# One encoder layer on one core: the first norm by wide VectorE operations, the first modulation rows behind the eighth state-space pair, and the up pass's input factors two attention blocks sooner

## The chip, the cores and the metric

The kernel runs on one core of a Trainium2 chip. A core has five engines with an instruction queue each: TensorE (PE: matmuls, with PEld for its weight loads), VectorE (DVE), ScalarE (ACT), GpSimd (POOL) and SyncE (SP), which here only issues DMAs. Every engine works through its own queue in order, and an instruction whose operand is not ready holds back all that is queued behind it. The metric is device time in microseconds (us); less is better.

## The reference, cut to what matters

One layer (depth 1), 2048 positions, 1024 channels, one sequence:

```
mod = c @ w_ada + b_ada                       # six rows of 1024: shift, scale, gate, twice
h = rms_norm(x, g_pre_mix) * (1 + sc_m) + sh_m
u, f, q, k, v = split(h @ w_in)
y = concat(s5_mixer(u), fourier_mixer(f), window_attention(q, k, v)) @ w_out
x = x + gt_m * rms_norm(y, g_post_mix)
h = rms_norm(x, g_pre_ffn) * (1 + sc_f) + sh_f
gate, val = split(dwconv3(h @ w_up))
x = x + gt_f * rms_norm((gelu(gate) * val) @ w_down, g_post_ffn)
```

The s5 mixer is a diagonal complex state-space scan over 24 channel groups in two directions with a gated output. The attention sees 128 positions to either side, with 6 query heads on 2 key heads.

## The kernel before, in words

**Layout and precision.** Channels lie on the 128 partitions, in 8 chunks of 128; positions are the free axis, mostly in four chunks c of 512. Large products run in split fp16: a value is written as HI + LO, and a product takes three matmuls (HI*HI, LO*HI, HI*LO). So what feeds TensorE is made twice, as a HI by ScalarE and as a LO (the value less its HI) by VectorE.

**Order of the work.** Nothing is ordered by hand. Each step is a Python generator (a process) that asks for an engine with an assumed cost and a ready time; `Sched` (line 121) is a greedy planner: of all processes that could go it takes the one that can start earliest on the planned clocks, ties going to the smaller priority number, and lets it emit its instruction. Each engine's queue gets its order from those planned times. `("w", future)` makes a process wait in the plan until another has set the future; `("acq", sem, n)` takes places of a limited resource, a PSUM bank for example. Such a gate is no instruction: it only decides how early in the queues the steps behind it stand. The planner books a VectorE tensor_tensor at 0.07 + 0.00105 us per element of a partition and a GpSimd one at 0.07 + 0.0022 us. It knows nothing of engines that slow each other down.

**Buffers.** All working tiles (`u`, 4 KB for each partition) come out of one pool of 50. PSUM has three groups of banks: z (3), s (4), m (1).

**Stages.**
1. Modulation: `mod_scale` (line 359) makes the first scale by matmuls, `mod_shift` (line 394) makes the first shift by eight wide multiply-and-sum rows on VectorE. When both are there for channel chunk k, the future `f_as[k]` is set.
2. First norm, `norm_x(c)` (line 479), for c = 0 to 3: four loads of x, squares on ScalarE, sums, a matmul by ones and an inverse root (`rnorm`, line 344). Then for each k the value x * r * a1 + s1 is made and split into HI and LO. For an even k this is `affine_split` (line 464): two VectorE scalar_tensor_tensor and one ScalarE activation of 512 each. For an odd k it is `affine_split2` (line 471): a GpSimd tensor_tensor by r, two ScalarE activations and a VectorE subtraction. `f_h[k][c]` is set when both halves lie there. Chunks 1 to 3 wait for `f_as[7]`.
3. The input projection (`ustream`, `zstream`) reads these halves; the constants of the s5 mixer (`s5_consts`, line 728) are made on VectorE, GpSimd and ScalarE next to it.
4. Twelve s5 pairs, prepared by `s5_prep` and run by two `s5_chain` processes (line 954). Pair b sets `f_yd[b]`.
5. The other 32 modulation rows, `mod_rest` (line 430). Each is one 512 KB load by SyncE (line 265) and one VectorE multiply-and-sum of 1024 (line 444), at the lowest priority. Rows 0 to 7 give `gm` (used by `proj`), 8 to 15 `s2`, 16 to 23 `a2` (used by `post`, which waits for `f_modr`), 24 to 31 `gf` (used at the end). Rows 8 to 23 wait for `f_yd[7]`, rows 24 to 31 for the first output projection tile; with `G_M1 = 0` rows 0 to 7 wait for nothing but `f_as[7]`.
6. Fourier mixer, gate of the s5 output, and attention in 16 blocks by two workers (`att`, line 1275; block n sets `f_ya[n]`), all of attention's matmuls in s banks. Output projection `proj` (line 1412) for c = 0 to 3, each needing four attention blocks, and `post` (line 1474), the second norm, which sets `f_hp[c]`.
7. The up pass (`ffn`, line 1652) in two halves p of the positions. The convolution is folded into a fast product scheme with seven products for each weight; `hcomb(p)` (line 1562) makes the seven input factors H of half p: per half 8 wide VectorE sums or differences and 14 HI and LO splits of 2 x 512. For p = 0 it waits for `f_hp[0]` and `f_hp[1]`, and, as `H_GATE = 1`, for `f_ya[15]`, the last attention block. `ffn` then walks over 22 weight tiles; for each it takes a place, two `u` tiles (line 1678) and an s bank, and only then waits for its H factor. The first weights are prepared after `f_pc[0]`, the end of the first output projection chunk's matmuls.
8. The down pass, of the same product scheme, and the last norm.

Lines 270, 275, 282, 284, 289, 305 and 316 are the helpers that emit ScalarE activations, tensor_tensor, tensor_scalar (282 and 284), scalar_tensor_tensor, memset and matmuls. All steps share them, so the profile is read by time and shape more than by line.

Of the kernel before, what the change touches and what calls it, by code (L numbers as in the profile page):

```python
# [12 lines left out]
AF = mybir.ActivationFunctionType  # L13
ALU = mybir.AluOpType
X = mybir.AxisListType.X

P = 128
# [20 lines left out]
HI, LO = 0, 1  # L38
# [4 lines left out]
PK = 100  # L43
S5_MUL = "V"
S5_ADD = "V"
G_M1 = 0
POST_B = 0.0
S5_B = 0.0
ATT_B = 0.0
# [20 lines left out]
N_SL = 3  # L70
W_ADD, H_ADD, G_ADD, SSQ = "VVVV", "V", "VVVV", "V"
W_LEAD, W_RAW, U_PAIRS, D_LEAD, TAIL = 3, 1, 4, 6, 2
F_GATE, H_GATE, D_FROM = 0, 1, (1, 0, 2)
N_CH = 2
N_PE = (1,)
G_M2 = 8
# [126 lines left out]
class Builder:  # L203
# [257 lines left out]
                self.f_gf.set(t)  # L461


    def affine_split(self, t, x, r, a, b, hi, lo):

        t = yield from self.stt(t, x, x, a, r, ALU.mult, ALU.mult)
        t = yield from self.act(t, hi, x, AF.Identity, bias=b)
        t = yield from self.stt(t, lo, x, b, hi, ALU.add, ALU.subtract)
        return t

    def affine_split2(self, t, x, r, a, b, hi, lo):

        t = yield from self.tt(t, x, x, r, ALU.mult, eng="G")
        t = yield from self.act(t, hi, x, AF.Identity, scale=a, bias=b)
        t = yield from self.act(t, x, x, AF.Identity, scale=a, bias=b)
        t = yield from self.tt(t, lo, x, hi, ALU.subtract)
        return t

    def norm_x(self, c, slots):
        t0 = yield ("acq", slots, 1)  # L480
        if c:
# [1 line left out]
        xs, tx = [], []  # L483
        for q in range(4):
            x = self.u([2, 512])
# [3 lines left out]
        for q in range(4):  # L489
            sq.append(self.u([2, 512]))  # L490
            if (c, q) in SQ_G:
                t = yield from self.tt(tx[q], sq[q], xs[q], xs[q], ALU.mult, eng="G")
            else:
                t = yield from self.act(tx[q], sq[q], xs[q], AF.Square)
# [6 lines left out]
        if c not in N_PE:  # L501
            acc = sq[0]
            t = yield from self.tt(max(ts_), acc, acc, sq[2], ALU.add)
            t = yield from self.stt(t, acc[:, 0], acc[:, 0], DELTA, acc[:, 1], ALU.add, ALU.add)
            parts = [(t, acc[:, 0])]
        rt = self.u([2, 512])
        tr = yield from self.rnorm(parts, 512, rt[:, 0], rt[:, 1])
        h = self.h[c] = [[self.u([4, 512], F16) for _ in range(2)] for _ in range(2)]
        for q in range(4):
            for k in (2 * q, 2 * q + 1):  # L510
                ta = yield ("w", self.f_as[k])
                ta = yield from (self.affine_split2 if k % 2 else self.affine_split)(
                    max(tr, ta), xs[q][:, k % 2], rt[:, 0], self.a1[:, k:k + 1], self.s1[:, k:k + 1],
                    h[HI][k // 4][:, k % 4], h[LO][k // 4][:, k % 4])
                self.f_h[k][c].set(ta)
        slots.give(ta)
        if c:
# [1044 lines left out]
    def hcomb(self, p):  # L1562
# [1 line left out]
        for i in range(2):  # L1564
            yield ("w", self.f_hp[2 * p + i])
        (ya, ta), (yb, tb) = self.f_hp[2 * p].val, self.f_hp[2 * p + 1].val
        if p == 0 and H_GATE:
            yield ("w", self.f_ya[15])
        H = self.H[p] = {}
        if p:  # L1570
            self.f_ht = {r: [Fut(), Fut()] for r in (1, 5, 6, 2, 7, 3, 4)}
# [80 lines left out]
    def ffn(self):  # L1652
# [10 lines left out]
        self.f_wd = [Fut() for _ in range(11)]  # L1663
        self.sc.spawn(self.down_weights(), 4)
        pairs = Sem(U_PAIRS)
        for p in range(2):
            fH = self.f_H[2 * p]
            gos = {}
# [4 lines left out]
            for i in range(NFF):  # L1673
# [22 lines left out]
                t = yield ("acq", self.bank["s"], 1)  # L1696
                b1 = self.ps("s")
                t = yield from prod(1, b1, max(t, tp), True)
                self.sc.spawn(self.up_copy(t, b1, U[0][:, n0], f[1]))
                t = yield ("acq", self.bank["s"], 1)  # L1700
                b2 = self.ps("s")
                t = yield from prod(5, b2, t, True)
                self.sc.spawn(self.up_copy(t, b2, U[1][:, n1], f[5]))
                t = yield ("w", f[1])
                t = yield from prod(6, b1, t, False)
                self.sc.spawn(self.up_copy(t, b1, U[0][:, n1], f[6]))
                t = yield ("acq", self.bank["z"], 1)
                b3 = self.ps("z")
                t = yield from prod(2, b3, t, True)
                self.sc.spawn(self.up_add(t, b3, U[0][:, n0], f[1], f[2], True))  # L1710
                t = yield ("w", f[6])
                t = yield from prod(7, b1, t, False)
                self.sc.spawn(self.up_add(t, b1, U[1][:, n1], f[5], f[7], False))
                t = yield ("w", f[5])
                t = yield from prod(3, b2, t, False)
                self.sc.spawn(self.up_add(t, b2, U[0][:, n1], f[6], f[3], True))
                t = yield ("w", f[7])
# [392 lines left out]
```

## Time and profile before

| what | us |
| --- | --- |
| median of 3 runs | 2134.07 (2133.83 to 2138.75) |
| the profiled execution | 2141.4 |
| its span, first to last instruction | 2139.6 |
| TensorE busy in the span | 1963.9 (92%) |
| VectorE busy | 1559.8 (73%) |
| ScalarE busy | 991.0 (46%) |
| GpSimd busy | 244.6 (11%) |
| mean granted TensorE clock | 0.962 |

The profiled execution is 7.3 us above the median, so a sum made in its time is carried over to the median as a difference. A row of the timeline reads: start, length, engine, line, operation, output <- inputs with their shapes, how many are merged, and in brackets the idle time ahead of it and what ended that. A row of `windows` reads: stretch, its length, busy time of PE, PEld, DVE, ACT and POOL with the number of instructions, the granted clock, the DMA engines' share and GB/s.

### The profile page before, as it was taken

The page shows a single profiled execution, that of the slowest core. Times are in us where ns is not written, and L with a number is a line of the kernel's source. Part 1 is how long each engine was busy: PE and PEld are TensorE (multiplying, and loading weights), DVE is VectorE, ACT ScalarE, POOL GpSimd, SP SyncE. Part 2 cuts the span into 40 slices and gives each one's busy share as a digit, 9 for nine tenths or more (in the row PEclk, how much of TensorE's full clock was granted, in tenths as well). Part 3 has the DMA queues.
Part 4 walks back from the last instruction along what each step waited for, and adds up shares of the span by engine and source line. Part 5 has one row for each costly group of instructions (what it writes and reads, how often), then busy time and mean ns, then how long its engine had stood idle before and what let it go on. Part 6 is the DMA issues. An engine that isn't in the chain of part 4 may idle for free.

```text
span 2139.6 us, 26850 instructions
## 1 busy us (share of the span) xinstructions
PE 1963.9 (92%) x9796; PEld 967.3 (45%) x9796; DVE 1559.8 (73%) x2305; ACT 991.0 (46%) x1666; POOL 244.6 (11%) x310
## 2 busy tenths in 40 slices
PE   6788888789988889997999999999999999999997
PEld 1336764444543444443444444444444444434445
DVE  8998898869677767899988875666565763547356
ACT  3643333355566576665555543444444433322221
POOL 1566554002000000000000000000000000011002
PEclk9989999899999989998999999999999999999998
DMA  9362145673746333346655566656565494548533
GB/s 368 105 209 61 56 127 162 217 247 137 256 144 220 126 125 133 136 179 249 223 197 187 188 216 260 230 189 226 201 217 201 158 334 157 162 134 300 177 100 113
DMA packets 206663, 397.27 MB, mean 186 GB/s; under 512 B 19521, under 2 KB 111938, under 8 KB 206530
## 3 DMA queue, kind: packets, MB, share of 16 engines
q1 hardware_dynamic: 206530, 395.55, 53.7%
q8 instruction: 77, 1.26, 0.2%
q14 instruction: 56, 0.46, 0.1%
HBM read 258.93 MB, written 134.98 MB: 184 GB/s over the span
## 4 chain that ended last, share of the span: by engine, by line
PE 49%; DVE 8%; ACT 2%; issue 1%; DMA 1%; POOL 0%; SPq 0%; POOLq 0%; DVEq 0%; ACTq 0%
PE ps L316 49%; DVE u L289 4%; DVE u L275 3%; ACT u L270 2%; DMA u<-d 0%; DMA u<-w_up 0%; DMA d<-u 0%; ACT L270 0%; POOL u L275 0%; SPq L265 0%; POOLq L2095 0%; DVE u L282 0%; ACT c L270 0%; DVEq L289 0%; DVEq L275 0%
## 5 line engine op out<-in xcount | busy, mean ns | idle before, releaser
L316 PE MATMUL ps<-u,u 128*128 128x512 f16 (+5 forms) x9030 | 1879.2, 368 | 90.7 <-DVE u L289 40.5
L316 PEld LDWEIGHTS <-u 128*128 128x128 f16 (+1 forms) x9058 | 846.8, 99 | 1035.4 <-issue 157.6
L275 DVE TENSOR_TENSOR u<-u,u 128x512 f32<-128x512 f32 (+10 forms) x584 | 506.6, 900 | 105.9 <-ACT u L270 92.4
L270 ACT ACTIVATE u<-u 128x1024 f16<-128x1024 f32 (+7 forms) x485 | 406.0, 869 | 360.9 <-DVE u L275 150.3
L270 ACT ACTIVATE u<-ps 128x512 f32<-128x512 f32 (+8 forms) x497 | 268.7, 555 | 410.4 <-PE ps L316 377.5
L289 DVE SCALAR_TENSOR_TENSOR u<-u,c,u 128x1023 f32<-128x1023 f32 (+5 forms) x248 | 291.3, 1197 | 61.2 <-ACT u L270 53.9
L289 DVE SCALAR_TENSOR_TENSOR u<-ps,u 128x512 f32<-128x512 f32 (+4 forms) x231 | 152.3, 666 | 229.2 <-PE ps L316 199.2
L289 DVE SCALAR_TENSOR_TENSOR u<-u,u 128x1024 f16<-128x1024 f32 (+6 forms) x225 | 240.6, 1093 | 61.4 <-ACT u L270 58.1
L275 POOL TENSOR_TENSOR u<-u,u 128x288 f32<-128x288 f32 (+9 forms) x169 | 187.4, 1123 | 609.3 <-DVE u L289 462.4
L270 ACT ACTIVATE u<-u,c 128x1023 f32<-128x1023 f32 (+3 forms) x106 | 123.5, 1166 | 142.5 <-DVE u L289 122.7
L305 POOL MEMSET u<- 128x1 f32 x88 | 8.6, 98 | 1118.0 <-DVE u L289 415.8
L270 ACT ACTIVATE u<-u,st 128x384 f32<-128x384 f32 (+3 forms) x192 | 107.5, 592 | 30.8 <-DVE st L282 17.3
L316 PEld LDWEIGHTS ps<-u,u 128*128 128x128 f32 (+1 forms) x532 | 91.1, 180 | 39.9 <-DVE u L275 16.8
L316 PE MATMUL ps<-u,c 128*128 128x512 f32 (+4 forms) x142 | 61.8, 551 | 43.5 <-DVE u L300 18.5
L316 PE MATMUL ps<-c,u 128*128 128x128 f16 (+1 forms) x568 | 59.6, 229 | 23.9 <-ACT u L270 18.5
L270 ACT ACTIVATE c<-u 128x2 f32<-128x2 f32 (+1 forms) x88 | 17.8, 202 | 132.3 <-DVE u L289 132.2
L275 DVE TENSOR_TENSOR u<-u 128x512 f32<-128x512 f32 (+8 forms) x136 | 67.8, 502 | 12.4 <-ACT u L270 11.6
L300 DVE TENSOR_TENSOR_SCAN u<-u,u 128x512 f32<-128x512 f32 (+1 forms) x60 | 68.6, 1152 | 0.5
L1330 DVE CUSTOM_DVE_ANT_0 u<-ps,u 128x384 f32<-128x384 f32 (+1 forms) x96 | 48.1, 536 | 23.8 <-PE ps L316 23.7
L289 DVE SCALAR_TENSOR_TENSOR u<-u,st,u 128x384 f16<-128x384 f32 (+1 forms) x96 | 54.6, 603 | 12.2 <-ACT u L270 12.0
L270 ACT ACTIVATE u<-u,c,c 128x512 f32<-128x512 f32 (+1 forms) x64 | 48.4, 804 | 22.3 <-DVE u L275 6.2
L316 PEld LDWEIGHTS ps<-u,c 128*128 128x128 f32 (+1 forms) x142 | 23.9, 190 | 72.6 <-issue 46.6
(52 smaller groups left out, 370.9 us busy)
## 6 DMA issues: line engine op xcount, KB each, us to landing
u<-d SPq DMA_DIRECT2D x226, 512.0 KB
d<-u SPq DMA_DIRECT2D x158, 512.0 KB
d<-u SPq DMA_DIRECT2D x111, 256.0 KB
u<-w_ada SPq DMA_DIRECT2D x48, 512.0 KB
u<-w_up SPq DMA_DIRECT2D x44, 512.0 KB
u<-d SPq DMA_DIRECT2D x66, 256.0 KB
u<-x SPq DMA_DIRECT2D x32, 512.0 KB
u<-d SPq DMA_DIRECT2D x24, 511.0 KB
```

Source lines behind the costliest of these rows:

```text
L270: self.S.activation(out, in_, func, **kw)
L275: (self.V if eng == "V" else self.G).tensor_tensor(out, a, b, op)
L289: self.V.scalar_tensor_tensor(out, a, s, b, op0, op1)
L300: self.V.tensor_tensor_scan(out, d0, d1, 0.0, ALU.mult, ALU.add)
L305: (self.V if eng == "V" else self.G).memset(out, v)
L316: self.PE.matmul(o, a, b, start=st, stop=sp, skip_group_check=chain)
L1330: V.tensor_tensor_reduce(out=s_, in0=o, in1=self.bias[h // 2][:, h % 2, bo:bo + nk * 128], op0=ALU.add, op1=ALU.max, scale=1.0, scalar=-3e ...
```

## The change

Three things change.

- **First norm.** `affine_split` and `affine_split2` go. For each pair of channel chunks q, one VectorE tensor_tensor multiplies [2, 512] by r in place (r broadcast over the pair), four ScalarE activations of 512 make HI and then the full value in place for both k, and one VectorE tensor_tensor of [2, 512] makes both LO. GpSimd has no part in it any more. `f_h` is set for both chunks of a pair at once.
- **First modulation rows.** `G_M1` is 8, so that rows 0 to 7 wait for `f_yd[7]` like rows 8 to 23.
- **Up pass.** `H_GATE` is 13: `hcomb(0)` waits for `f_ya[13]` and not for `f_ya[15]`. `ffn` itself now waits for `f_ya[15]` before its walk over the weights, so it takes its first two `u` tiles and its first s bank there.

```diff
--- before.py
+++ after.py
@@ -43,7 +43,7 @@
 PK = 100
 S5_MUL = "V"
 S5_ADD = "V"
-G_M1 = 0
+G_M1 = 8
 POST_B = 0.0
 S5_B = 0.0
 ATT_B = 0.0
@@ -70,7 +70,7 @@
 N_SL = 3
 W_ADD, H_ADD, G_ADD, SSQ = "VVVV", "V", "VVVV", "V"
 W_LEAD, W_RAW, U_PAIRS, D_LEAD, TAIL = 3, 1, 4, 6, 2
-F_GATE, H_GATE, D_FROM = 0, 1, (1, 0, 2)
+F_GATE, H_GATE, D_FROM = 0, 13, (1, 0, 2)
 N_CH = 2
 N_PE = (1,)
 G_M2 = 8
@@ -461,21 +461,6 @@
                 self.f_gf.set(t)
 
 
-    def affine_split(self, t, x, r, a, b, hi, lo):
-
-        t = yield from self.stt(t, x, x, a, r, ALU.mult, ALU.mult)
-        t = yield from self.act(t, hi, x, AF.Identity, bias=b)
-        t = yield from self.stt(t, lo, x, b, hi, ALU.add, ALU.subtract)
-        return t
-
-    def affine_split2(self, t, x, r, a, b, hi, lo):
-
-        t = yield from self.tt(t, x, x, r, ALU.mult, eng="G")
-        t = yield from self.act(t, hi, x, AF.Identity, scale=a, bias=b)
-        t = yield from self.act(t, x, x, AF.Identity, scale=a, bias=b)
-        t = yield from self.tt(t, lo, x, hi, ALU.subtract)
-        return t
-
     def norm_x(self, c, slots):
         t0 = yield ("acq", slots, 1)
         if c:
@@ -507,11 +492,16 @@
         tr = yield from self.rnorm(parts, 512, rt[:, 0], rt[:, 1])
         h = self.h[c] = [[self.u([4, 512], F16) for _ in range(2)] for _ in range(2)]
         for q in range(4):
+            t = yield from self.tt(tr, xs[q], xs[q], rt[:, 0:1].to_broadcast([P, 2, 512]), ALU.mult)
+            hi, lo = (h[x][q // 2][:, 2 * (q % 2):2 * (q % 2) + 2] for x in range(2))
+            for j in range(2):
+                k = 2 * q + j
+                ta = yield ("w", self.f_as[k])
+                ab = dict(scale=self.a1[:, k:k + 1], bias=self.s1[:, k:k + 1])
+                ta = yield from self.act(max(t, ta), hi[:, j], xs[q][:, j], AF.Identity, **ab)
+                ta = yield from self.act(ta, xs[q][:, j], xs[q][:, j], AF.Identity, **ab)
+            ta = yield from self.tt(ta, lo, xs[q], hi, ALU.subtract)
             for k in (2 * q, 2 * q + 1):
-                ta = yield ("w", self.f_as[k])
-                ta = yield from (self.affine_split2 if k % 2 else self.affine_split)(
-                    max(tr, ta), xs[q][:, k % 2], rt[:, 0], self.a1[:, k:k + 1], self.s1[:, k:k + 1],
-                    h[HI][k // 4][:, k % 4], h[LO][k // 4][:, k % 4])
                 self.f_h[k][c].set(ta)
         slots.give(ta)
         if c:
@@ -1564,8 +1554,8 @@
         for i in range(2):
             yield ("w", self.f_hp[2 * p + i])
         (ya, ta), (yb, tb) = self.f_hp[2 * p].val, self.f_hp[2 * p + 1].val
-        if p == 0 and H_GATE:
-            yield ("w", self.f_ya[15])
+        if p == 0:
+            yield ("w", self.f_ya[H_GATE])
         H = self.H[p] = {}
         if p:
             self.f_ht = {r: [Fut(), Fut()] for r in (1, 5, 6, 2, 7, 3, 4)}
@@ -1663,6 +1653,7 @@
         self.f_wd = [Fut() for _ in range(11)]
         self.sc.spawn(self.down_weights(), 4)
         pairs = Sem(U_PAIRS)
+        yield ("w", self.f_ya[15])
         for p in range(2):
             fH = self.f_H[2 * p]
             gos = {}
```

## The prediction

> **What bounds the kernel now.** I read the page first, then stretches, then groups and single rows.
>
> ```profile
> span 2139.6 us, 26850 instructions
> PE   6788888789988889997999999999999999999997
> DVE  8998898869677767899988875666565763547356
> POOL 1566554002000000000000000000000000011002
> ```
>
> ```profile
> 60.00:160.00 100.00, 79.10 (x307) 33.74 (x306) 95.56 (x133) 52.34 (x73) 62.57 (x55) 0.88 0.46 151
> 160.00:460.00 300.00, 251.39 (x1517) 171.60 (x1516) 252.97 (x436) 108.38 (x211) 127.80 (x124) 0.93 0.45 141
> 600.00:840.00 240.00, 206.14 (x1201) 106.02 (x1200) 166.56 (x361) 162.47 (x342) 0.00 (x0) 0.92 0.46 155
> 900.00:1080.00 180.00, 162.64 (x729) 71.94 (x728) 170.29 (x182) 112.33 (x158) 1.97 (x20) 0.96 0.56 210
> ```
>
> TensorE is the bound of the kernel as a whole, so a gain can only come out of its idle time, and that lies early. From 60 to 160 us it idles 20.9 of 100 while VectorE is busy 95.6: norms and s5 constants wait in VectorE's queue. From 160 to 460 (s5 pairs) TensorE idles 48.6 and VectorE is 84% busy: a relay between the two. From 900 to 1080, the start of the up pass, TensorE idles 17.4 with VectorE 95% busy. Behind 1080 this change touches nothing.
>
> **Part 1, the first norm.** Its present price is three groups between 20 and 170 us, 16 instructions each, one for each pair of channel chunks and each position chunk:
>
> ```profile
> L289 DVE SCALAR_TENSOR_TENSOR u<-u,c,u 128x512 f32<-128x512 f32 x16 | 19.7, 1253 | 0.0
> L289 DVE SCALAR_TENSOR_TENSOR u<-u,c,u 128x512 f16<-128x512 f32 x16 | 16.2, 1020 | 0.0
> L275 DVE TENSOR_TENSOR u<-u,u 128x512 f16<-128x512 f32 x16 | 15.3, 964 | 0.5 <-ACT u L270 0.5
> L444 DVE CUSTOM_DVE_ANT_0 u<-u,u 128x1024 f32<-128x1024 f32 x8 | 9.8, 1222 | 0.2 <-DMA u<-w_ada 0.2
> L275 DVE TENSOR_TENSOR u<-u,u 128x1024 f32<-128x1024 f32 x4 | 6.3, 1581 | 3.2 <-ACT u L270 3.2
> L444 DVE DVE_READ_ACCUMULATOR2_ANT c<- 128x1 f32 x8 | 0.7, 86 | 0.0
> ```
>
> That is 19.7 + 16.2 + 15.3 = 51.2 us of VectorE. The new form has 16 products and 16 subtractions of 1024. Their clean price stands where hcomb runs with GpSimd idle, and the price beside GpSimd is the 1.581 us above:
>
> ```profile
> 840.25 10.30 DVE L275 TENSOR_TENSOR u<-u,u 128x1024 f32<-128x1024 f32 x9
> 858.67 4.63 DVE L275 TENSOR_TENSOR u<-u,u 128x1024 f16<-128x1024 f32 x4
> ```
>
> Clean: 16 x 1.144 + 16 x 1.158 = 36.8, saving 14.4 us. Always beside GpSimd: 32 x 1.581 = 50.6, saving 0.6. Why the old forms are so dear shows in GpSimd's own row:
>
> ```profile
> 24.19 4.99 POOL L275 TENSOR_TENSOR u<-u,u 128x512 f32<-128x512 f32 x4 [12.08 <-issue]
> ```
>
> ```profile
> L275 POOL TENSOR_TENSOR u<-u,u 128x512 f32<-128x512 f32 x12 | 20.7, 1751 | 10.9 <-DVE u L289 10.9
> ```
>
> The same operation takes 4.99 / 4 = 1.25 us in the first position chunk and 1.75 in the other three (60 to 130 us), when VectorE is full: the two slow each other down. Removing 16 of them takes away most of that. What is left on GpSimd (three sums of squares, constants) still stretches some, so I take 12 of the 14.4.
>
> ScalarE pays:
>
> ```profile
> L270 ACT ACTIVATE u<-u,c,c 128x512 f16<-128x512 f32 x16 | 12.6, 807 | 15.8 <-POOL u L275 5.7 <-DVE c L275 5.7 <-DVE c L284 4.5
> L270 ACT ACTIVATE u<-u,c 128x512 f16<-128x512 f32 x16 | 11.5, 717 | 28.4 <-DVE u L289 26.8 <-DVE c L284 1.5
> 896.11 15.70 PE L316 MATMUL ps<-u,u 128*128 128x512 f16 x72
> ```
>
> For a pair 4 x 0.807 = 3.23 in place of 0.717 + 2 x 0.807 = 2.33, so 16 x 0.90 = 14.4 us more, in a stretch where it is 52% busy. A position chunk then takes ScalarE 4 x 3.23 = 12.9 us, but the u tiles of that chunk are 72 matmuls, 15.7 us, so TensorE still covers it: nothing. Without that cover (TensorE waiting for h at every chunk) it costs 4 x 0.90 = 3.6 a chunk. Setting `f_h` by pairs costs the first chunk nine matmuls of lateness, 2 us, which the next row hides, a 6.2 us wait of TensorE soon after:
>
> ```profile
> 79.56 6.54 PE L316 MATMUL ps<-u,u 128*128 128x512 f16 x21 [6.20 <-DVE u L289]
> ```
>
> **Part 2, the eight rows.** They leave 9.8 + 0.7 = 10.5 us of VectorE before 160 us, and the last stands directly ahead of the operation behind which the s5 pairs begin:
>
> ```profile
> 145.17 1.23 DVE L444 CUSTOM_DVE_ANT_0 u<-u,u 128x1024 f32<-128x1024 f32 x1
> 146.66 0.42 DVE L284 TENSOR_SCALAR u<-u,c 128x384 f32<-128x384 f32 x1
> ```
>
> So the pairs start 12 + 10.5 = 22.5 us sooner. I let that pass whole to their end, since VectorE leads the relay.
>
> The rows come back behind `f_yd[7]`, with all they issue: 8 loads of 512 KB on SyncE, moved past the s5 pairs' transfers, and 10.5 us of VectorE. The present 16 gated rows run from the first to the second of these rows, and the results are needed by the others:
>
> ```profile
> 334.67 1.72 DVE L444 CUSTOM_DVE_ANT_0 u<-u,u 128x1024 f32<-128x1024 f32 x1
> 477.13 1.22 DVE L444 CUSTOM_DVE_ANT_0 u<-u,u 128x1024 f32<-128x1024 f32 x1
> 565.24 0.67 ACT L270 ACTIVATE u<-ps,c 128x512 f32<-128x512 f32 x1
> 612.45 0.67 ACT L270 ACTIVATE u<-ps,c 128x512 f32<-128x512 f32 x1
> ```
>
> One row in (477.13 - 334.67) / 15 = 9.5 us. From 334.67 - 22.5 = 312 on, the eighth comes at 379 (gm, needed by the first evacuation, now at 565) and the 24th at 531 (post needs it when the first chunk's eight tiles are out, now at 613, then some 595). Both are covered, by over 160 and by 60 us. On VectorE, between nothing and 10.5 us of them falls into the relay before the pairs end, where it has 16% of room; I take the middle, 5. Front in sum: -22.5 + 5 = -17.5, between -26 (14.4 + 10.5 and a little of the others' stretch) and +13 (0.6 from the norm, the rows back in full, 13.8 lost by the first rival).
>
> **Part 3, the up pass.** `hcomb(0)` is the 9 rows' 10.3 us above and 15 splits at 1.158, 27.7 us of VectorE. For p = 0 it issues no DMA. It could start at the first of these rows (block 13) instead of the second (block 15); its other input, the second chunk's norm, ends 40 us before:
>
> ```profile
> 815.47 0.55 DVE L289 SCALAR_TENSOR_TENSOR u<-ps,u 128x384 f16<-128x384 f32 x1
> 839.78 0.56 DVE L289 SCALAR_TENSOR_TENSOR u<-ps,u 128x384 f16<-128x384 f32 x1 [3.02 <-ACT u L270]
> 766.66 5.74 ACT L270 ACTIVATE u<-u,c,c 128x512 f32<-128x512 f32 x8
> 815.00:840.00 25.00, 21.67 (x144) 11.86 (x143) 17.18 (x47) 18.67 (x45) 0.00 (x0) 0.93 0.63 219
> 839.79 49.80 PE L316 MATMUL ps<-u,u 128*128 128x512 f16 x229 [0.58 <-ACT u L270]
> ```
>
> H is not late today: TensorE runs 49.8 us without a gap behind block 15. What the move can give is VectorE's backlog at the start of the up pass, and only as much as VectorE idles in those 25 us: 25 - 17.2 = 7.8. The remaining 19.9 stands ahead of the last two blocks' own operations, and behind those wait the last output projection and, by the new gate, the whole up pass. At worst block 15 ends 19.9 later and the up pass gets back its 17.4 of idle: +2.5. At best -7.8. I take -5.
>
> The gate in `ffn` also takes away a hold: from the first prepared weight on, `ffn` keeps an s bank and two buffers while it waits for H, so attention has three banks of four. TensorE's waits there:
>
> ```profile
> PE ps L316 <- ACT u L270: 18.4, 15, 11.6
> PE ps L316 <- DVE u L282: 5.6, 4, 3.9
> 978.77 21.27 PE L316 MATMUL ps<-u,u 128*128 128x512 f16 x84 [10.70 <-DVE u L289]
> ```
>
> Only the 5.6 behind L282 are surely waits for a bank being emptied; between 0 and -5.6, I take -1.5. The new waits are gates of the plan, so no engine's queue stands behind them.
>
> The longest gap of the up pass is the last row: 10.70 idle, then 84 matmuls at 253 ns against 15.70 / 72 = 218 before. The Trainium skill ("TensorE: Matmul & The Clock Gate", Part 1: The HAM clock gate (the "warmup" mystery)) says that TensorE's clock is halved after an idle window of some 3.4 us and has to be earned back. By that rule each long gap that closes gives more than its length, here 84 x 35 ns = 3 us more, and the sum would be 3 larger; I leave it out. The trace agrees as far as it goes: a granted clock of 0.96 in that stretch.
>
> Sum: -17.5 - 5 - 1.5 = -24, so 2141.4 goes to 2117.4, and the median 2134.1 to **2110**.
>
> **The rivals.**
>
> *The contention moves to the s5 constants (2124).* GpSimd makes 24 small products for them, of which these are the first and the last:
>
> ```profile
> 110.82 1.82 POOL L275 TENSOR_TENSOR u<-u 128x48 f32<-128x48 f32 x2 [1.57 <-ACT u L270]
> 127.25 4.61 POOL L275 TENSOR_TENSOR u<-u,u 128x336 f32<-128x336 f32 x4
> ```
>
> A VectorE operation of 1024 lasts twice one of 512. If each small product waits half of 1.15 us longer, 24 x 0.575 = 13.8 us, the constants and with them the pairs come only 8.7 sooner: -8.7 + 5 - 6.5 = -10. For it: 0.9 us for a product of 48 elements is a wait already. Against: with the rows gone they start sooner and beside fewer norms. The Trainium skill ("SBUF — State Buffer", SBUF: two separate sides) has such a rule: VectorE with two SBUF inputs and GpSimd share a port pair, and whoever starts first holds it for the whole instruction. The 1.75 against 1.25 us above agrees.
>
> *The rows take back what the front gave (2133).* The loading stretch is full:
>
> ```profile
> 420.00:440.00 20.00, 18.37 (x133) 12.07 (x132) 16.61 (x27) 6.44 (x11) 0.00 (x0) 0.97 0.78 268
> SPq L265 <- DVE u L275: 92.1, 21, 15.7
> ```
>
> 8 x 0.524 MB at 268 GB/s are 15.6 us; one behind the other with 10.5 of VectorE that is 26.1 against 22.5, +3.6, and with part 3 about -1.5. Against: rows are the last in priority and have 60 us of cover.
>
> *SyncE's queue is held (2146).* A row's load waits at the head of SyncE's queue for its buffer, and loads of pairs, tables and attention wait behind. SyncE's waits for VectorE between 30 and 440 us average 92.1 / 21 = 4.4 us, the longest 15.7. Eight at 4.4 are 35, net of 22.5 and 6.5 +6; with one at 15.7 it is 46.5, net +17.5; the middle is +12. It decides from 29 / 8 = 3.6 us a row. Against: fewer transfers stand behind it once the pairs are through.
>
> *The up part does nothing or no sooner (2117).* Only the front is left, -17.5.
>
> **How the numbers follow.** Forecast 0.55, contention 0.15, rows 0.13, SyncE 0.12, front alone 0.05. A run can tell 0.3%, 6.4 us, from no change. Faster is the first, second and last, 0.75; same 0.13; slower 0.12. The low end is all three parts at their best ends, -26 - 7.8 - 5.6, about -40; the high end lies just over the third case: 2094 to 2138.
>
> **What would show it.** Right: the three groups replaced by 32 operations near 1.15; the s5 pairs beginning near 125, not 147; the last attention block near 820; under 12 us of idle TensorE in the up pass's first 180 us. Wrong: wide operations near 1.58, pairs starting after 136, the s5 pairs' end less than 10 us sooner, or attention's last two blocks over 10 us longer.

## The result, and the profile after

| what | before | after |
| --- | --- | --- |
| median of 4 runs each, on one chip | 2136.41 | 2159.2 |
| ratio, with its 95% interval | | 1.0107 (1.0082 to 1.0133) |
| the profiled execution | 2141.4 | 2156.83 |
| its span | 2139.6 | 2155.1 |

The change makes the kernel about 23 us slower where the forecast had it 24 us faster. First the line of busy time after, then three stretches and, among them, the two 20 us pieces in which the loss shows:

```profile
PE 1964.1 (91%) x9796; PEld 969.6 (45%) x9796; DVE 1540.2 (71%) x2289; ACT 1004.5 (47%) x1682; POOL 203.6 (9%) x294
```

```profile
60.00:160.00 100.00, 91.61 (x394) 44.59 (x393) 89.11 (x150) 66.05 (x98) 47.01 (x53) 0.93 0.37 120
160.00:460.00 300.00, 250.69 (x1510) 168.95 (x1509) 254.71 (x454) 110.98 (x218) 114.76 (x124) 0.94 0.46 148
...
820.00:840.00 20.00, 1.59 (x2) 0.65 (x3) 19.11 (x25) 12.62 (x13) 0.00 (x0) 0.55 0.00 1
840.00:860.00 20.00, 6.55 (x33) 2.85 (x32) 17.02 (x30) 12.77 (x28) 0.00 (x0) 0.50 0.26 92
900.00:1080.00 180.00, 167.86 (x753) 74.57 (x752) 157.82 (x169) 105.97 (x149) 1.97 (x20) 0.97 0.53 196
```

VectorE has 19.6 us less to do (1559.8 before) and GpSimd 41.0 less, ScalarE 13.5 more: the work changed as intended. From 60 to 160 us TensorE is 12.5 us busier than before, and from 900 to 1080 us it idles 12.1 instead of 17.4. But from 820 to 860 us it works 8.1 of 40 us. That is one hole, and the timeline of VectorE says what fills it:

```profile
807.57 0.55 DVE L289 SCALAR_TENSOR_TENSOR u<-ps,u 128x384 f16<-128x384 f32 x1
...
814.79 0.56 DVE L289 SCALAR_TENSOR_TENSOR u<-ps,u 128x384 f16<-128x384 f32 x1 [0.17 <-ACT u L270]
815.27 4.75 DVE L275 TENSOR_TENSOR u<-u,u 128x1024 f16<-128x1024 f32 x4
820.63 17.12 DVE L275 TENSOR_TENSOR u<-u,u 128x1024 f16<-128x1024 f32 x15 [0.62 <-ACT u L270]
...
838.27 0.42 DVE L1320 CUSTOM_DVE_ANT_0 u<-ps,u 128x256 f32<-128x256 f32 x1
...
864.94 0.56 DVE L289 SCALAR_TENSOR_TENSOR u<-ps,u 128x384 f16<-128x384 f32 x1 [2.00 <-ACT u L270]
```

The first two rows are the last evictions of attention blocks 13 and 14, the last row that of block 15. Between them stand the sums and splits of `hcomb(0)`, the rows of 1024 (a merged row has the shape of its first instruction); only behind them come the evictions of block 15's scores (128x256), the first step of its long chain. In the kernel before, the first score of block 15 and the last eviction of block 14 are these:

```profile
815.93 0.42 DVE L1330 CUSTOM_DVE_ANT_0 u<-ps,u 128x256 f32<-128x256 f32 x1
...
832.75 0.55 DVE L289 SCALAR_TENSOR_TENSOR u<-ps,u 128x384 f16<-128x384 f32 x1
```

TensorE after the change, in the time of the hole:

```profile
811.00 8.10 PE L316 MATMUL ps<-u,u 128*128 128x512 f16 x47
838.41 2.07 PE L316 MATMUL ps<-u,c 128*128 128x512 f32 x2 [19.31 <-DVE u L275]
...
851.94 1.19 PE L316 MATMUL ps<-c,u 128*128 128x128 f16 x6 [10.60 <-DVE u L275]
...
859.51 7.35 PE L316 MATMUL ps<-u,u 128*64 128x384 f16 x29 [1.07 <-DVE u L282]
```

It waits 19.31 and 10.60 us and has nothing else: the last output projection needs block 15, and so, by the new gate, does the whole up pass. Block 14 ended 18.0 us sooner than before (814.79 for 832.75), block 15 25.2 us later (864.94 for 839.78), so this place costs 43.1 us against the front's 18.0. From block 15's end to the end of the span, 9.7 us come back.

The front, in the groups of VectorE between 20 and 170 us and in the start of the s5 pairs:

```profile
L275 DVE TENSOR_TENSOR u<-u,u 128x1024 f32<-128x1024 f32 x20 | 26.7, 1343 | 3.7 <-ACT u L270 3.7
L275 DVE TENSOR_TENSOR u<-u,u 128x1024 f16<-128x1024 f32 x16 | 19.8, 1243 | 0.5 <-ACT u L270 0.5
```

```profile
124.20 10.46 POOL L275 TENSOR_TENSOR u<-u,u 128x336 f32<-128x336 f32 x9
...
132.95 2.86 DVE L275 TENSOR_TENSOR u<-u,u 128x256 f32<-128x256 f32 x4 [6.56 <-POOL u L275]
```

The 16 products (here in one group with four older sums) and 16 subtractions take about 16 x 1.343 + 19.8 = 41.3 us where the old norm took 51.2. The pairs begin at 133 us, and now VectorE waits 6.56 us for GpSimd ahead of them. In the kernel before, the same operations begin at 147.54:

```profile
147.54 3.32 DVE L275 TENSOR_TENSOR u<-u,u 128x256 f32<-128x256 f32 x4
```

The last short scan of the pairs shows their end, before and after:

```profile
418.32 0.28 DVE L300 TENSOR_TENSOR_SCAN u<-u,u 128x64 f32<-128x64 f32 x1
```

```profile
382.22 0.29 DVE L300 TENSOR_TENSOR_SCAN u<-u,u 128x64 f32<-128x64 f32 x1
```

So the pairs end 36 us sooner, and at block 14 only 18 us of that are left. This needs an explanation too.

### The profile page after: what moved, and what is told of

The parts are those of the page before. It is cut to its first block, busy times and chain, and to the rows that moved or that the text cites. A ratio compares the mean times of both kernels' runs of the same rounds, so it can differ in the third digit from the quotient of the medians.

```text
span 2155.1 us, 26806 instructions
## 1 busy us (share of the span) xinstructions
PE 1964.1 (91%) x9796; PEld 969.6 (45%) x9796; DVE 1540.2 (71%) x2289; ACT 1004.5 (47%) x1682; POOL 203.6 (9%) x294
## 4 chain that ended last, share of the span: by engine, by line
PE 52%; DVE 8%; ACT 3%; issue 2%; DMA 1%; SPq 0%; POOL 0%; POOLq 0%; DVEq 0%; ACTq 0%
PE ps L316 52%; DVE u L289 4%; DVE u L275 4%; ACT u L270 2%; DMA u<-d 1%; ACT L270 0%; DMA u<-w_up 0%; SPq L265 0%; DVE u L282 0%; POOL u L275 0%; ACT c L270 0%; DVE u L1320 0%; POOLq L2086 0%; ACT st L270 0%; DVEq L289 0%
## 5 line engine op out<-in xcount | busy, mean ns | idle before, releaser
L316 PE MATMUL ps<-u,u 128*128 128x512 f16 (+7 forms) x9030 | 1874.4, 368 | 77.6 <-ACT u L270 27.4
L275 DVE TENSOR_TENSOR u<-u,u 128x512 f32<-128x512 f32 (+11 forms) x600 | 529.8, 916 | 115.5 <-ACT u L270 89.9
L270 ACT ACTIVATE u<-u 128x1024 f16<-128x1024 f32 (+9 forms) x485 | 406.6, 869 | 387.0 <-DVE u L275 157.5
L270 ACT ACTIVATE u<-ps 128x512 f32<-128x512 f32 (+7 forms) x497 | 269.2, 555 | 395.2 <-PE ps L316 367.0
L289 DVE SCALAR_TENSOR_TENSOR u<-u,c,u 128x1023 f32<-128x1023 f32 (+4 forms) x216 | 255.6, 1205 | 63.6 <-ACT u L270 58.2
L289 DVE SCALAR_TENSOR_TENSOR u<-u,u 128x1024 f16<-128x1024 f32 (+7 forms) x225 | 240.1, 1088 | 57.6 <-ACT u L270 52.9
L275 POOL TENSOR_TENSOR u<-u,u 128x288 f32<-128x288 f32 (+10 forms) x153 | 151.6, 1003 | 591.2 <-DVE u L289 468.3
L270 ACT ACTIVATE u<-u,c 128x1023 f32<-128x1023 f32 (+2 forms) x90 | 111.9, 1245 | 114.5 <-DVE u L289 95.9
L270 ACT ACTIVATE u<-u,st 128x384 f32<-128x384 f32 (+3 forms) x192 | 107.8, 593 | 22.7 <-DVE st L282 17.9
L316 PE MATMUL ps<-c,u 128*128 128x128 f16 (+1 forms) x568 | 63.6, 238 | 33.0 <-ACT u L270 14.9
L270 ACT ACTIVATE u<-u,c,c 128x512 f32<-128x512 f32 (+1 forms) x96 | 71.4, 803 | 15.5 <-DVE c L284 8.5
```

The costliest lines, as they stand in the source:

```text
L270: self.S.activation(out, in_, func, **kw)
L275: (self.V if eng == "V" else self.G).tensor_tensor(out, a, b, op)
L289: self.V.scalar_tensor_tensor(out, a, s, b, op0, op1)
L316: self.PE.matmul(o, a, b, start=st, stop=sp, skip_group_check=chain)
```

## The experiments

**The theories.** Theory 1: the up pass's part is the loss. In the plan `hcomb` has priority 0 and attention 0.5 (`P_ATT`), so once `f_ya[13]` is set every tie on VectorE goes to the splits; block 15, whose worker has just finished 13, gets ready at the same moment and stands behind all of them. Theory 2, its rival: the front, whose new times re-order the plan, is the loss, and block 15 is late only because of that. Theory 3: the wait in `ffn`, which keeps the up pass out, is what costs.

**First set.** `h_only` is the kernel before with the up pass's part alone:

```diff
-F_GATE, H_GATE, D_FROM = 0, 1, (1, 0, 2)
+F_GATE, H_GATE, D_FROM = 0, 13, (1, 0, 2)
...
-        if p == 0 and H_GATE:
-            yield ("w", self.f_ya[15])
+        if p == 0:
+            yield ("w", self.f_ya[H_GATE])
...
+        yield ("w", self.f_ya[15])
```

> The kernel before with the up pass's part alone (H_GATE 13 and the wait of ffn on the last attention block); norm and rows as before. Theory 1 (hcomb(0) wins every tie on VectorE against block 15 in the plan, because its priority is 0 against 0.5; block 15 then ends alone with TensorE dry, and the up pass gives back only some 10 us): 2150 to 2175, block 15's last eviction 25 to 45 us later than the 839.8 of before. Theory 2 (the front is the loss, and block 15's lateness in the changed kernel comes from its re-ordered plan): 2128 to 2143, block 15's last eviction within 10 us of before.

Measured: 2158.1, ratio 1.0097 (1.0077 to 1.0117). The rows in which its block 15 waits:

```profile
824.55 0.42 DVE L1330 CUSTOM_DVE_ANT_0 u<-ps,u 128x256 f32<-128x256 f32 x1
...
824.89 19.38 DVE L275 TENSOR_TENSOR u<-u,u 128x1024 f16<-128x1024 f32 x17
844.20 0.68 DVE L275 TENSOR_TENSOR u<-u 128x512 f32<-128x512 f32 x1
844.80 0.41 DVE L1330 CUSTOM_DVE_ANT_0 u<-ps,u 128x256 f32<-128x256 f32 x1
...
867.71 0.56 DVE L289 SCALAR_TENSOR_TENSOR u<-ps,u 128x384 f16<-128x384 f32 x1 [1.29 <-ACT u L270]
```

One score of block 15 is evicted, then 17 operations of `hcomb(0)`, then the rest; the block ends 27.9 us later than before. Nearly the whole loss is there with an unchanged front.

`front_only` is the changed kernel with `H_GATE = 1` and no wait in `ffn`.

> The changed kernel with the norm and the eight rows as changed, but the up pass as before (hcomb(0) behind block 15, no wait in ffn). Theory 1: the front gains what block 14 shows in the changed kernel, some 18 us, so 2108 to 2125, with block 15's last eviction near 820. Theory 2: 2140 or more, block 15 not ahead of 835.

Measured: 2140.0, ratio 1.0008 (0.9994 to 1.0021), block 15's last eviction at 836.84. These are the figures that theory 2 expected, but its claim does not follow: within the interval the front is no loss to speak of. Nor is theory 1's 18 us there: the front's gain does not reach the end. Front and up part add up: 1.0008 x 1.0097 = 1.0105 against 1.0107.

`h_low_prio` is the changed kernel with one edit:

```diff
-            self.sc.spawn(self.hcomb(p), 0)
+            self.sc.spawn(self.hcomb(p), 0 if p else 0.6)
```

> The changed kernel whole, with hcomb(0) spawned at priority 0.6 in place of 0, so that attention (0.5) goes first where both could start. Theory 1: block 15's score evictions are mixed with the splits, block 15 ends within 10 us of block 14's 815 or so, and the time falls to 2100 to 2128. Theory 2: 2145 or more, since the front and not the order of these ties is the loss.

Measured: 2139.3, ratio 1.0009 (0.9999 to 1.0020). Block 15's scores are now evicted between 818.5 and 826.9 us, mixed with the splits, and 20 of the 23 us are gone, so the ties are needed for the loss. Neither theory had the number right. The time did not fall to 2128, since block 15 still ends 33 us behind block 14 (850.22 and 817.37), and since the front gives nothing.

`gate_only` is the kernel before with the wait in `ffn` alone.

> The kernel before with one line more: ffn waits for block 15 before its walk. Theory 1: an s bank that is no longer held is worth 0 to 5, and nothing else moves: 2128 to 2140. Theory 3 (the missing early start of the weight walk is what costs): 2145 or more, with TensorE idle right behind block 15.

Measured: 2139.8, ratio 1.0010 (0.9997 to 1.0024). The wait does no harm where no splits stand ahead of block 15. In its trace TensorE idles 12.5 us from 900 to 1080 us where it idled 17.4, and the 10.70 us gap there is 4.34. But in `rows_only` below, whose up pass is as before, the same figures are 12.7 and 4.61. So the smaller idle time of the changed kernel (12.1) is no sign of an earlier H, nor of this wait.

`h_no_gate` is the changed kernel without that wait, so with the splits ahead of block 15 but the up pass free to start.

> The changed kernel without the wait of ffn on block 15 (H_GATE 13 kept). Theory 1 (the ties on VectorE between hcomb(0) and block 15 are the loss): the hole stays, but ffn may begin its first products in it: 2140 to 2160. Theory 3 (the wait is what keeps TensorE dry in the hole): 2125 to 2140.

Measured: 2141.3, ratio 1.0020 (1.0010 to 1.0029). Here are VectorE's rows from its hole and TensorE's in the same place:

```profile
831.17 2.36 DVE L275 TENSOR_TENSOR u<-u,u 128x1024 f16<-128x1024 f32 x2 [0.22 <-ACT u L270]
833.45 0.42 DVE L1320 CUSTOM_DVE_ANT_0 u<-ps,u 128x256 f32<-128x256 f32 x1
...
834.14 8.17 DVE L275 TENSOR_TENSOR u<-u,u 128x1024 f32<-128x1024 f32 x7
```

```profile
825.33 19.28 PE L316 MATMUL ps<-u,u 128*128 128x512 f16 x83 [2.56 <-DVE u L275]
844.77 9.79 PE L316 MATMUL ps<-u,u 128*128 128x512 f16 x47 [0.15 <-DVE u L289]
```

Two of block 15's six scores are evicted at 833 us, the others between 847 and 869, behind sums and splits and now also behind the up pass's own steps, and it ends only at 940 us. Still 18 us are won back: TensorE multiplies for the up pass meanwhile. (The 2141.3 lies in theory 1's range and just above theory 3's.) So theory 1 named half of it and theory 3 the other half. The splits make block 15 late, and the wait leaves TensorE nothing to do until it comes. The wait alone (`gate_only`) and the splits alone (here, with the changed front) cost 4 us or less, the two together 20.

**Second set: where the front's gain goes.** TensorE does the same matmuls in every kernel, so its busy time summed from the start is a first measure of how far the work has come. Stretches of `windows` from 0, first the kernel before, then `front_only`:

```profile
0.00:120.00 120.00, 84.42 (x286) 31.54 (x287) 108.67 (x224) 63.00 (x83) 46.34 (x38) 0.90 0.64 234
0.00:480.00 480.00, 385.84 (x2012) 225.92 (x2013) 414.05 (x783) 199.85 (x351) 196.77 (x188) 0.91 0.52 173
0.00:640.00 640.00, 535.78 (x2905) 301.00 (x2906) 541.03 (x1055) 295.35 (x558) 209.71 (x202) 0.93 0.52 174
0.00:800.00 800.00, 670.37 (x3674) 369.77 (x3675) 654.00 (x1292) 403.34 (x775) 209.71 (x202) 0.93 0.51 171
0.00:880.00 880.00, 747.00 (x4098) 407.98 (x4099) 715.62 (x1396) 453.90 (x868) 209.91 (x204) 0.93 0.50 167
```

```profile
0.00:120.00 120.00, 91.84 (x335) 35.73 (x336) 102.61 (x234) 83.19 (x109) 15.52 (x23) 0.93 0.66 240
0.00:480.00 480.00, 396.32 (x2142) 232.86 (x2143) 408.96 (x777) 222.11 (x388) 163.98 (x182) 0.94 0.51 176
0.00:640.00 640.00, 532.88 (x2873) 300.17 (x2874) 531.28 (x1042) 307.07 (x562) 168.47 (x186) 0.94 0.52 180
0.00:800.00 800.00, 678.35 (x3761) 376.85 (x3762) 644.15 (x1302) 421.88 (x811) 168.47 (x186) 0.94 0.50 172
0.00:880.00 880.00, 746.20 (x4103) 408.96 (x4104) 708.14 (x1389) 469.78 (x890) 168.67 (x188) 0.94 0.50 170
```

The differences of the first busy column are TensorE's lead over the kernel before. Worked out in the same way for the others:

| kernel, time against before | 120 us | 480 | 640 | 800 | 880 |
| --- | --- | --- | --- | --- | --- |
| after, 1.0107 | 7.4 | 10.3 | -2.2 | 7.9 | -21.6 |
| h_only, 1.0097 | -0.8 | -2.4 | -2.4 | -5.4 | -20.4 |
| front_only, 1.0008 | 7.4 | 10.5 | -2.9 | 8.0 | -0.8 |
| h_no_gate, 1.0020 | 8.6 | 14.1 | -1.6 | 10.4 | 10.7 |
| norm_only, 1.0137 | 7.8 | 2.0 | -18.4 | -8.5 | -23.4 |
| before_book, 1.0159 | -0.1 | -1.0 | -6.7 | -18.0 | -23.4 |
| front_book, 0.9952 | 1.1 | 12.0 | 11.7 | 11.9 | 9.7 |

Busy time has a flaw as a measure, since a matmul at a lower granted clock counts for longer: to 480 us the clock was 0.91 before and 0.94 in `front_only`, and over the whole span the same matmuls come to between 1957.7 (`all_book`) and 1977.2 us (`before_book`). So the matmuls themselves have to be counted. These are the ones of the most frequent shape to 480 us, before and then in `front_only`:

```profile
L316 PE MATMUL ps<-u,u 128*128 128x512 f16 x753 | 194.1, 411 | 31.4 <-DVE u L289 16.7 <-DVE u L275 10.3 <-ACT u L270 4.3
```

```profile
L316 PE MATMUL ps<-u,u 128*128 128x512 f16 x834 | 201.3, 391 | 13.8 <-ACT u L270 8.7 <-DVE u L289 2.8 <-DVE u L275 2.2
```

81 more of them are done, in 7.2 us more of busy time; two neighbours of this shape start 0.216 us apart (the median of all traces), so the 81 are 17.5 us of work. With every shape counted in this way, the lead over the kernel before in us of finished matmuls is:

| kernel | 120 us | 480 | 640 | 800 | 880 | 2100 | span shorter by |
| --- | --- | --- | --- | --- | --- | --- | --- |
| after | 11.0 | 19.8 | 2.8 | 10.2 | -22.7 | -15.5 | -15.5 |
| front_only | 10.4 | 21.5 | 2.8 | 14.3 | 1.5 | 6.0 | 6.2 |
| norm_only | 10.6 | 11.3 | -11.4 | -12.4 | -30.5 | -25.9 | -25.8 |
| before_book | 3.7 | 6.1 | -2.7 | -28.2 | -37.6 | -34.3 | -34.2 |
| front_book | 1.3 | 20.7 | 17.0 | 14.9 | 11.4 | 13.9 | 13.7 |

At 2100 us this lead agrees with the difference of the spans. So the front is some 20 us ahead at 480, twice what busy time says, though not 36. The lead is lost from 480 to 640, comes back, and is lost again around 840, where in `front_only` block 15 runs alone from 811 to 837 us and TensorE is busy 37.9 of the 50 us from 800. Theory A: the chain of attention blocks sets the end of that part and the lead is idled away. Theory B: one half of the front loses what the other gains. `norm_only` is `front_only` with `G_M1 = 0`, `rows_only` the kernel before with `G_M1 = 8`:

> The kernel before with the changed norm alone. The front with norm and rows took 2140.0 against 2136.7 although its s5 pairs began 14 us sooner; its TensorE had done 7 us more matmul time at 120 us and none more at 840. Theory A (what the front gains is work that TensorE only does sooner, and the chain of attention blocks, not TensorE, sets when block 15 ends, so the gain is idled away again): 2131 to 2143, with the TensorE lead again below 2 us at 840. Theory B (the norm's gain is real and the moved rows eat it): 2120 to 2130.

> The kernel before with rows 0 to 7 behind the eighth pair alone. Theory A: 2131 to 2143, for the same reason. Theory B (the rows are the loss): 2143 to 2152.

Measured: `norm_only` 2166.0, ratio 1.0137 (1.0122 to 1.0151); `rows_only` 2135.6, ratio 0.9993 (0.9983 to 1.0003). On the kernel before, the rows are neutral. The norm alone is 29 us slower, although its TensorE leads by 7.8 us of busy time at 120: both theories fail on it. With the rows added to this norm (`front_only`) the loss is gone, so the two parts do not add up.

To fill the hole of block 15, the last output projection chunk was let start on three attention blocks, with its s5 and Fourier rows first:

```diff
-            for f in self.f_ya[4 * c:4 * c + 4]:
+            for f in self.f_ya[4 * c:4 * c + (4 if c < 3 else 3)]:
...
-                for i, k in enumerate((5, 6, 7, 3, 4, 0, 1, 2)):
+                for i, k in enumerate((5, 6, 7, 3, 4, 0, 1, 2) if c < 3 else (3, 4, 0, 1, 2, 5, 6, 7)):
...
-                        tk = ta
+                        tk = yield ("w", self.f_ya[4 * c + 3])
+                        tk = max(ta, tk)
```

> The changed norm and rows, up pass as before, and one edit more: the last output projection chunk waits for three attention blocks in place of four, sums its s5 and Fourier rows first and waits for block 15 only ahead of the attention rows, so TensorE has up to 3 tiles x 15 matmuls, some 10 us, to do while block 15 runs alone. Theory A: the front's 8 us of lead at 800 us are no longer idled away, so 2127 to 2134, TensorE more than 45 of 50 busy from 800 to 850 where the front alone has 37.9. Rival (the lead is lost elsewhere, or the early projection takes banks and buffers from attention): 2137 or more.

> The control: the same edit of the last output projection on the kernel before, whose blocks 14 and 15 end together and whose TensorE is 46.7 of 50 busy from 800 to 850. Theory A: 2131 to 2140, clearly less gain than in the front kernel. Rival (the fill is worth as much without the front): the same gain as in the front kernel, then it says nothing on where the front's lead went.

Measured: 2138.5 for both, ratios 1.0009 (0.9998 to 1.0019) and 1.0007 (0.9997 to 1.0017). That is the rival's figure. The hole was filled (44.9 of 50 us busy from 800 in the front kernel), but the end did not move: its lead in busy time at 800 was by then 3.8 and not 8.0. One hole less was another elsewhere, so this pair does not tell where the lead goes.

**Third set: the order.** A first hint is the distance of attention's fifth block from the fourth. Last evictions of blocks 3 and 4 (from 0) of the kernel before:

```profile
548.57 0.56 DVE L289 SCALAR_TENSOR_TENSOR u<-ps,u 128x384 f16<-128x384 f32 x1 [3.99 <-ACT u L270]
...
583.92 0.56 DVE L289 SCALAR_TENSOR_TENSOR u<-ps,u 128x384 f16<-128x384 f32 x1 [0.17 <-ACT u L270]
```

and of `norm_only`:

```profile
538.69 0.56 DVE L289 SCALAR_TENSOR_TENSOR u<-ps,u 128x384 f16<-128x384 f32 x1 [1.50 <-ACT u L270]
...
649.76 0.55 DVE L289 SCALAR_TENSOR_TENSOR u<-ps,u 128x384 f16<-128x384 f32 x1
```

35 us in one, 111 in the other; in `front_only` 50 (532.41 and 582.78). The fifth block needs q projections of the second position chunk and a Fourier output, and when these stand in the queues is for the planner to say. Its bookings: a scalar_tensor_tensor of 512 costs 0.13 + 0.538 us, a tensor_tensor of 512 0.07 + 0.538 and one of 1024 1.145. By these the old norm takes 16 x (2 x 0.668 + 0.608) = 31.1 us of VectorE and the new one 32 x 1.145 = 36.6. So in the plan VectorE's part of the norm gets 5.5 us longer, on the chip 9.9 us shorter, and all later work is laid out for a clock that moves the wrong way. (ScalarE's 16 more activations are booked at 0.63 us each as well.) Theory A': this re-ordering, not the new instructions, decides what becomes of the front. `before_book` changes no instruction of the kernel before: 0.115 us are added to the booked cost of the norm's 48 VectorE steps. `front_book` is `front_only` with lower bookings:

```diff
-            t = yield from self.tt(tr, xs[q], xs[q], rt[:, 0:1].to_broadcast([P, 2, 512]), ALU.mult)
+            t = yield ("V", 0.85, tr)
+            self.V.tensor_tensor(xs[q], xs[q], rt[:, 0:1].to_broadcast([P, 2, 512]), ALU.mult)
+            t += self.LAT
```

and the same for the subtraction (0.85) and the activations (0.45).

> The kernel before with not one instruction changed: only the costs that the planner books for the 48 VectorE steps of the first norm are 0.115 us each higher, 5.5 us in all, about what the new norm's booking adds. Theory A' (the front's result is set by the order that the planner makes out of its bookings: they put Fourier, q projections and attention behind each other in another way; here it puts the second chunk's q projections far later): 2150 to 2175. Rival (the order of so much later work is robust, and the losses come from the new instructions): 2130 to 2143.

> The changed norm and rows, up pass as before, every instruction as in the front kernel: only the planner books the wide norm operations at 0.85 in place of 1.145 us and its ScalarE steps at 0.45 in place of 0.63, so that its clock runs about as with the old norm and it orders the q projections and the attention much as before. Theory A': the front's gain on the chip, some 8 to 14 us of TensorE's lead, now reaches the end: 2118 to 2131. Rival (attention's own chain idles the lead away in any order): 2133 to 2145.

Measured: `before_book` 2171.8, ratio 1.0159 (1.0141 to 1.0177); `front_book` 2127.2, ratio 0.9952 (0.9938 to 0.9967). The fourth and fifth block of `before_book`:

```profile
536.65 0.55 DVE L289 SCALAR_TENSOR_TENSOR u<-ps,u 128x384 f16<-128x384 f32 x1
...
660.99 0.55 DVE L289 SCALAR_TENSOR_TENSOR u<-ps,u 128x384 f16<-128x384 f32 x1
```

5.5 us of booking cost 35 us with not one instruction changed, and put the fifth block 124 us behind the fourth. With lower bookings, which give an order near that of before (the fifth block 44 us behind the fourth), the same new instructions are 10 us faster than before, and of 20.7 us of lead at 480 there are 13.9 left at 2100. Theory A' holds: the order alone takes 35 us in one kernel and gives some 12 in another. For `norm_only` itself no run has other bookings, and `front_book` lowers VectorE's and ScalarE's at once, so which of the two counts was not separated.

`before_book` also answers what the 36 us at the pairs' end were: its pairs begin at 150.31, later than before, and their last short scan is at 387.62, 31 us sooner than before, with no instruction changed. So most of that milestone's move can come from the order, and it says little about time won. `front_book2` has bookings of 0.4 and 0.3 instead of 0.85 and 0.45, and nearly the same order:

> front_book with the norm booked still lower (0.4 us for a wide operation, 0.3 for a ScalarE step), which gives nearly the same order of the later work. If the order decides: within 4 us of front_book's 2127.2. If front_book's gain came from a lucky detail of its bookings: back at 2134 to 2143.

Measured: 2134.5, ratio 0.9978 (0.9968 to 0.9988): faster than before, 7 us over `front_book`, outside the 4 us given. So an order near the old one lets the front's gain through, and how much, 3 to 13 us by the two intervals, still hangs on details of the order. The trace shows where the 7 us go: ahead of its first pair VectorE waits 23.49 us for TensorE (until 155.55), so the first scan of 512 is at 158.38 us for 147.80 in `front_book`, and block 15's last eviction at 835.51 for 828.58.

**Last: is an early H worth anything?** `all_book` is the changed kernel with the bookings of `front_book` and `hcomb(0)` at 0.6; `book_low_no_gate` also leaves out the wait in `ffn`.

> The changed kernel whole, with both cures: the norm booked as in front_book, and hcomb(0) at priority 0.6 so that attention wins the ties. Theory A' with theory 1: as front_book or up to 5 us below it, 2115 to 2131. Rival: 2135 or more.

> The changed kernel with the norm booked as in front_book, hcomb(0) at priority 0.6 and without ffn's wait on block 15. all_book (the same with the wait) took 2129.6 and front_book (up pass as before) 2127.2. If an early H is worth something once neither the ties nor the wait are in its way: 2112 to 2124. If TensorE was full behind block 15 already and the gain goes into later gaps: 2124 to 2132, as front_book.

Measured: `all_book` 2129.6, ratio 0.9966 (0.9953 to 0.9978), inside its range; `book_low_no_gate` 2144.8, ratio 1.0030 (1.0020 to 1.0041), slower than both ranges that were expected for it. Neither beats `front_book`, where H comes behind block 15. Without the wait, in `book_low_no_gate`, the gap of the up pass is as long as ever:

```profile
980.46 7.79 PE L316 MATMUL ps<-u,u 128*128 128x512 f16 x27 [10.69 <-DVE u L289]
```

An early H moves splits out of the up pass's start and still does not shorten that gap, and block 15, with splits mixed into its chain, ends there 36 us behind block 14 (850.25 and 814.21). That this lateness is what makes it slower was not tested. The best version found is the new norm and rows with the bookings of `front_book` and the old up pass: 2127.2, faster than both kernels.

## Why the prediction was wrong

**Where TensorE idles, and part 1.** Right in mechanism: the three groups went and VectorE saved 51.2 - 41.3 = 9.9 us, near the 12 taken. The group means are 1.343 and 1.243 us and not 1.15, for two reasons. The 1.144 and 1.158 are the length of a merged row by its count, in which one operation starts before the last has ended; in the same view as the 1.343 the clean price is 1.223 and 1.222 (last section), so the clean saving was some 2 us less than the 14.4. And three of the operations were held up by GpSimd, one of them to 3.39 us. The 1.581 taken for "always beside GpSimd" was a mean too, of two operations held up (1.61 and 2.28 us) and two at 1.21 and 1.23. ScalarE's 13.5 us are the 14.4 expected; from 60 to 160 us TensorE was busier, so that cover held.

**Part 2.** The pairs began 14.6 us sooner, not 22.5. VectorE itself was there 21.2 us sooner (at 126.4), near the forecast, and then waited 6.56 us for GpSimd. This is not the first rival's mechanism: from the start of the first to the end of the last, the 24 small products took 19.1 us, and 21.0 before. What VectorE waited for were three products of 768 elements, which GpSimd ran ahead of the 24 in the kernel before (from 103.18 us) and behind them now (to 132.92): the order again. The rows were covered as argued: `rows_only` is neutral, and the first evacuation, which needs gm, came 21 us sooner (544.35 for 565.24) and waited for TensorE. SyncE's waits for VectorE fell to 65.7 us in 24, 2.7 each and below the 3.6 from which that rival decides (its waits for ScalarE rose from 84.6 to 115.5).

**The step that failed in the front** is the sum "Front in sum: -22.5 + 5 = -17.5", which takes what the pairs gain for what the kernel gains. "I let that pass whole to their end" came out (though, as `before_book` shows, the order alone can do nearly as much): the pairs ended 36 us sooner, and TensorE was some 20 us of matmuls ahead at 480 us. But a milestone is not the end, and what became of these 20 us was decided by the order of the later work. The front came out at a ratio of 1.0008, no difference that can be told, instead of -17.5 us. I read the plan's gates, but not what the change books in the plan; the bookings stood in the code, and 31.1 against 36.6 could have been worked out.

**The step that failed in part 3** is "At worst block 15 ends 19.9 later and the up pass gets back its 17.4 of idle: +2.5". Taken alone the part cost 21 us (1.0097). Both halves of that bound were wrong. Counted from block 13's last eviction, block 15 ended 57.4 us later where it was 24.3 before: 33 us late, not 19.9 (and 43 when block 14 is the measure). Nearly all of it is its start: its first score is evicted 30.7 us behind block 13 instead of 0.5, with the splits in between, and from there its chain took 26.7 us for 23.9. So nothing shows of the 7.8 us that the bound took off for VectorE's idle time. (By the code `hcomb` has 8 sums and 14 splits, about 25 us; the prediction counted 9 and 15, 27.7.) And from 900 to 1080 us TensorE idled some 5 us less, not 17.4, which `rows_only` shows without any change to the up pass. Above all the bound priced only VectorE's displaced time and not what TensorE has left meanwhile. The same sentence that counted the gate as a gain of 1.5 us ("takes away a hold") overlooked that it takes away TensorE's only other work: without it the same late block costs 18 us less. "The new waits are gates of the plan, so no engine's queue stands behind them" was true and misleading, since a gate that delays a stage empties an engine as well as a wait does.

The clock is the one place where a rule of the Trainium skill bears on the hole. In it two fp32 matmuls of 512 columns take 2.07 us behind 19.31 us of idle time; in `h_no_gate` the same two, with no idle time ahead, take 1.02, and the granted clock of the hole's two pieces is 0.55 and 0.50:

```profile
821.11 1.02 PE L316 MATMUL ps<-u,c 128*128 128x512 f32 x2
```

The Trainium skill ("TensorE: Matmul & The Clock Gate", Part 1: The HAM clock gate (the "warmup" mystery)) says that the clock is halved after an idle window of some 3.4 us; the two rows agree with the halving. It adds little to the loss, since only 8.1 us of matmuls lie in the hole.

**The signs named beforehand** pointed right: attention's last two blocks became over 10 us longer, which was listed as "wrong". The pairs' start (133) and TensorE's idle time (12.1) fell between the figures for right and wrong. What had no place among the rivals was the two mechanisms found, ties in the plan and an order that follows from bookings.

Left open: which of the two needs of the fifth block, q or Fourier, is the late one in `norm_only` and `before_book`, and why TensorE comes later to the first pair in `front_book2`.

## What to carry to other kernels

When work is pulled ahead of the last step that gates a stage, list what the gated engine can do until that step is through, and give the pulled work a lower priority than the step; a gate and an early start that are each harmless can cost 20 us together. Where a planner orders the queues from assumed costs, work out what a change does to its bookings as well as to the chip, and run the old instructions with the new bookings as a control. Measure progress by the work that the bound engine has finished at fixed times, not by when a stage ends; count its operations by shape, since busy time alone was off by half here where the granted clock differed.

## What had not been expected of the hardware

GpSimd did not stretch the wide VectorE operations evenly. Of the 36 between 20 and 170 us after the change, 33 took 1.21 to 1.23 us. That is the price of the same shapes where `hcomb` runs with GpSimd idle, here in the kernel before from 839 to 880 us:

```profile
L275 DVE TENSOR_TENSOR u<-u,u 128x1024 f32<-128x1024 f32 x17 | 20.6, 1223 | 0.5 <-ACT u L270 0.5
L275 DVE TENSOR_TENSOR u<-u,u 128x1024 f16<-128x1024 f32 x14 | 16.8, 1222 | 0.6 <-ACT u L270 0.6
```

Only five of the 36 met an instruction of GpSimd. Three began well inside one, and took 1.60, 1.62 and 3.39 us. The longest, and the GpSimd product that had begun 1 us ahead of it:

```profile
67.76 3.39 DVE L275 TENSOR_TENSOR u<-u,u 128x1024 f32<-128x1024 f32 x1
```

```profile
66.75 3.31 POOL L275 TENSOR_TENSOR u<-u,u 128x1024 f32<-128x1024 f32 x1 [6.29 <-ACT u L270]
```

All three ended 1.08 or 1.09 us behind GpSimd's product (this one at 71.15 and 70.06), as if nearly all of their work came after it. The other two began first and took their 1.22 and 1.21 us; there it was a GpSimd product of 48 elements, begun 0.2 and 0.1 us later, that took 1.12 and 1.27 us and ended some 0.14 behind VectorE, where others of its size took 0.28 to 0.55. In these five cases the one that came second seems to have waited for the first.
